# A router's gathering matrix from one comparison of counting products, with ranks and slots worked out afterwards

## The chip, the cores and the metric

The kernel runs on one core of a Trainium2 chip. The metric is the device time of one execution in microseconds (us); the time before is the median of three executions, 1223.32 us (1221.37 to 1224.46).

The engines of a core run their own instruction streams side by side and wait for each other through semaphores: TensorE (PE, matmuls; PEld is its weight load), VectorE (DVE), ScalarE (ACT), GpSimd (POOL) and SyncE (SP, which here only issues transfers). Transfers run on 16 DMA engines. PE writes its results to PSUM, DVE and ACT read them there and write to SBUF.

## The reference

One layer of a decoder trunk over 256 tokens of width 1024, all in float32. A token mixer (a gated linear attention branch and a short convolution branch) makes a new `x`. Then comes a mixture of experts:

```python
h   = RMSNorm(x) * (1 + scale2) + shift2
x   = x + gate2 * HierMoE(h)   # top-1 of 8 groups, then top-2 of 8 experts in the group
...
p_group = softmax(t @ rg_w + rg_b);  g_w, g_idx = top_k(p_group, 1)
e_logits = (t @ re_w + re_b).reshape(N, 8, 8)[group g_idx]
p_exp = softmax(e_logits);  e_w, e_loc = top_k(p_exp, 2)
e_w = e_w / sum(e_w) * g_w
out[token] += e_w * (silu(xb @ w1[e]) * (xb @ w3[e])) @ w2[e]
```

There are 64 experts of 6 MB of weights each (`w1`, `w3`: 1024 x 512, `w2`: 512 x 1024), and all of them are read. A final RMSNorm ends the layer.

## The kernel before

**The three stages.** First the token mixer (to about 297 us), whose weights come in blocks of 512 KB through a ring. Then the router: logits, top-1 group, top-2 experts, and for each token and choice a place in an expert's buffer. Then the experts, 16 groups of 4 experts (`EPG`), 12 units of 2 MB a group. Each expert has 32 slots (`CAP`), so that a group has 128 slots, one per column of a gathering matrix.

**The weight stream.** `Stream` holds the order of all transfers. SP issues the transfer of the next unit each time that the program is done with a unit (`st.done`) and so has a free buffer; the issue waits until PE has read the old unit for the last time. With all buffers asked for, eight transfers of 2 MB are outstanding at most.

**The router.** The logits are gathered in one PSUM tile (`pl`) by `x1_logits`, while the same blocks of `x` are transposed back to token rows; `ssq` holds the sums of squares. Then follow, as one chain of small operations: `rs` = 1/sqrt(mean square), logits `lg` = `pl` * `rs` + `rconst`, the maxima and their indices (`gm`, `gi`, `em`, `ei`), and `OO`, which holds for each token and choice a one at its expert (tokens x 2 halves x 2 choices x 64). ACT scales `acc` by `rs` to `h2`, the rows that will be gathered. The chain goes on:

- `osum` adds the two choices. Five small matmuls with `tri` (ones where the row is before the column) and `onesb` (ones) give `pc`: for each token and expert the number of tokens ahead that chose this expert, and in its third quarter the count of each expert.
- four instructions pick from `pc` the `rank` of each choice; `dst` = 32 * expert + rank (plus 8192 where the rank is 32 or more) is the place.
- two comparisons with a row of numbers (`io`) make `P1`, two more make and add `Pm`, the gathering matrix of group 0: tokens x 128 slots, a one where the token sits in the slot.
- `keep_warm` runs matmuls whose result nobody reads, 4 ahead of the counting matmuls and 2 behind them.

**Group 0.** Its eight first-layer units (`l1_unit`, u = 0 to 7) need the gathered columns `xg`; `gather_part` makes a quarter of them, four matmuls of `h2` with `Pm` into one PSUM tile and then two evacuations, which apply the norm's scale and shift: by ACT for the even quarters, by DVE for the odd ones. Quarter u is made just ahead of unit u for u = 0 to 3. After unit 3, `after_start` puts on DVE and ACT what the rest needs: the places in all groups (`dg`), `P1` of the second choice, the softmax weights (`weights`, six exponentials on ACT) and the tables for experts with more than 32 tokens (`overflow_tables`). After unit 5, `after_start2` makes the weighted matrix of group 0 by `slot_weights` (transposes on PE); it stands ahead of unit 6 on PE.

PSUM tiles named `m` come from a ring of four banks. One of the four holds `pl` until the experts begin; then the ring starts anew.

Of the kernel before, what the change touches and what calls it, by code (L numbers as in the profile page):

```python
# [27 lines left out]
LASTC = ((0, 512), (512, 256), (768, 128), (896, 128))  # L28
LASTN = (2, 2, 4, 4)
NB = 12  # L30
WARM = (4, 2)
# [65 lines left out]
def trunk_kernel(ctx: ExitStack, tc: tile.TileContext, xT: bass.AP, c: bass.AP, modw: bass.AP,  # L97
# [734 lines left out]
    assert not todo  # L832

    rs = sm.tile([128, 4], F32, name="rs")
    pl = L["pl"]
    V.tensor_reduce(rs[:, 2:4], ssq, axis=AX.X, op=OP.add)
    S.activation(rs[:, 0:2], rs[:, 2:4], AF.Sqrt, bias=epsc, scale=1.0 / D)
    V.reciprocal(rs[:, 0:2], rs[:, 0:2])
    o = [0]

    def scratch(*shape):
        n = 1
        for d in shape:
# [12 lines left out]
    OO = scratch(4, 64).rearrange("p (t k) e -> p t k e", t=2)  # L856
# [5 lines left out]
    xb, incl, excl = scratch(64), scratch(64), scratch(64)  # L862
    ovs = scratch(2, 2)
    cnt = scratch(64)
    osum = sm.tile([128, 2, 64], BF, name="osum")
# [13 lines left out]
    ebi = sm.tile([128, 3, 16], I32, name="ebi")  # L879

    for tt in range(TT):
        V.scalar_tensor_tensor(lg[:, tt], pl[:, tt, :72], rs[:, tt:tt + 1], rconst, op0=OP.mult, op1=OP.add)
    for tt in range(TT):
        V.max(gm[:, tt], lg[:, tt, :8])
    for tt in range(TT):
# [1 line left out]
    for tt in range(TT):  # L887
# [1 line left out]
    V.tensor_tensor(off8, io[:, None, :8].to_broadcast([128, 2, 8]), gi[:, :, 0:1].to_broadcast([128, 2, 8]),  # L889
                    op=OP.not_equal)  # L890
    V.scalar_tensor_tensor(lm.rearrange("p t (g e) -> p t g e", g=8), off8[:, :, :, None].to_broadcast([128, 2, 8, 8]),
                           -3.0e38, lg[:, :, 8:72].rearrange("p t (g e) -> p t g e", g=8), op0=OP.mult, op1=OP.add)
    for tt in range(TT):
        V.max(em[:, tt], lm[:, tt])
    for tt in range(TT):
        V.max_index(ei[:, tt], em[:, tt], lm[:, tt])
    V.tensor_tensor(OO, io[:, None, None, :64].to_broadcast([128, 2, 2, 64]),
                    ei[:, :, 0:2, None].to_broadcast([128, 2, 2, 64]), op=OP.is_equal)
    V.tensor_add(osum, O1, O2)
    V.tensor_scalar(dst, ei[:, :, 0:2], float(CAP), None, op0=OP.mult)  # L900
    keep_warm(WARM[0])
    pc = mt(4, 64)
    T.matmul(pc[:, 0], tri, osum[:, 0], start=True, stop=True)
    T.matmul(pc[:, 1], tri, osum[:, 1], start=True, stop=False)
    T.matmul(pc[:, 1], onesb, osum[:, 0], start=False, stop=True)
    T.matmul(pc[:, 2], onesb, osum[:, 0], start=True, stop=False)
    T.matmul(pc[:, 2], onesb, osum[:, 1], start=False, stop=True)
    keep_warm(WARM[1])
    for tt in range(TT):
        for k in range(2):  # L910
            V.scalar_tensor_tensor(prr[:, tt, k], pc[:, tt], 1.0, OO[:, tt, k], op0=OP.mult, op1=OP.mult,
                                   accum_out=rank[:, tt, k:k + 1])
    V.tensor_add(dst, dst, rank)
    V.tensor_scalar(big8, rank, float(CAP), 8192.0, op0=OP.is_ge, op1=OP.mult)
    V.tensor_add(dst, dst, big8)
    S.copy(cnt, pc[:, 2])
    pz_cm.__exit__(None, None, None)
    pa = ctx.enter_context(tc.tile_pool(name="pa", bufs=2, space=bass.MemoryType.PSUM))
    mring[:] = [(mring[0] + i) % 4 for i in range(4)]
    rot["m"] = 0  # L920

    def weights():
        V.tensor_scalar(nm[:, :, 0], gm[:, :, 0], -1.0, None, op0=OP.mult)
        V.tensor_scalar(nm[:, :, 1], em[:, :, 0], -1.0, None, op0=OP.mult)
        for tt in range(TT):
            S.activation(ex[:, 0:8], lg[:, tt, :8], AF.Exp, bias=nm[:, tt, 0:1], accum_out=zz[:, tt, 0:1])
            S.activation(ex, lm[:, tt], AF.Exp, bias=nm[:, tt, 1:2], accum_out=zz[:, tt, 1:2])
            S.activation(pw[:, tt], em[:, tt, 0:2], AF.Exp, bias=nm[:, tt, 1:2])
# [45 lines left out]
    def gather_part(xg, i):  # L974
        ps = mt(2, 128)
        for j in range(2):
            for tt in range(TT):
                f = 256 * i + 128 * j
                T.matmul(ps[:, j], h2[:, tt, f:f + 128], Pm[:, tt], start=(tt == 0), stop=(tt == 1))  # L979
        for j in range(2):  # L980
            k = 2 * i + j
            if i % 2 == 0:
                S.activation(xg[:, k], ps[:, j], AF.Identity, bias=B2[:, k:k + 1], scale=A2[:, k:k + 1])  # L983
            else:
                V.tensor_scalar(xg[:, k], ps[:, j], A2[:, k:k + 1], B2[:, k:k + 1], op0=OP.mult, op1=OP.add)  # L985

    def gather(key, i):
        X[key] = X["xg"][i % 2]
# [45 lines left out]
                T.matmul(ps[:, :w], pwt[:, tt], X["y"][:, s], start=True, stop=True)  # L1034
                V.tensor_add(acc[:, tt, s], acc[:, tt, s], ps[:, :w])  # L1035

    for tt in range(TT):
        V.tensor_scalar(P1[:, 0, tt], io, dst[:, tt, 0:1], None, op0=OP.is_equal)
    for tt in range(TT):
        V.scalar_tensor_tensor(Pm[:, tt], io, dst[:, tt, 1:2], P1[:, 0, tt], op0=OP.is_equal, op1=OP.add)  # L1040
    X["xg"] = [xt[:, i].rearrange("p (k s) -> p k s", k=KT) for i in range(2)]
    X["y"], X["g2r"] = xt[:, 2], xt[:, 3]
    X[0] = X["xg"][0]
# [63 lines left out]
    for g in range(NGRP):  # L1107
        if g == OVG:
            combine(g - 1)
            held = st.done(("e", g - 1, NU - 1), keep=True)  # L1110
            overflow(held)
            slots(g, dg, g)
            gather(g, g)
            slot_weights(g)
            st.free(held)
        ps = pa.tile([128, D], F32, name="a")
        for u in range(KT):
            if g == 0 and u < 4:
                gather_part(X[0], u)
            if g == last and u == 0:  # L1120
                S.dma_start(sq[0:1, :], bass.AP(tensor=fg.tensor, offset=fg.offset, ap=[[D, 1], [1, D]]))
            if g == last and u == 5:
                final_gain()
            l1_unit(ps, g, u, unit("e", g, u))
            st.done(("e", g, u))
            if g == 0 and u == 3:
                after_start()
            if g == 0 and u == 5:
                after_start2()
            if u == 2 and g > 0 and g != OVG:  # L1130
                combine(g - 1)
            if u == (4 if g else 6) and g + 1 < NGRP and g + 1 != OVG:
                slots(g + 1, dg, g + 1)
                gather(g + 1, g + 1)
                slot_weights(g + 1)
        act(ps)
        ps = pa.tile([128, D], F32, name="a")
        if g < last:
            for f in range(4):
                l2_unit(ps, f, unit("e", g, KT + f))  # L1140
                if not (g + 1 == OVG and f == 3):
                    st.done(("e", g, KT + f))
            evac_y(ps)
# [126 lines left out]
```

## Time and profile before

| | us |
|---|---|
| median of three executions | 1223.32 |
| the profiled execution | 1223.55 |
| its span | 1221.5 |
| PE busy | 907.0 (74%) |
| DVE busy | 378.1 (31%) |
| ACT busy | 224.2 (18%) |
| read from HBM over the span | 475.79 MB, 390 GB/s in the mean |

The span runs from the first to the last instruction on the engines. [...] In a row of the chain that ended last, a number is the start in us from the span's start and the next one how long this step held the end. In a row of a timeline the brackets say how long the engine sat idle before and what ended that.

### The profile page before, as it was taken

The page shows a single profiled execution, that of the slowest core. Times are in us where ns is not written, and L with a number is a line of the kernel's source. Part 1 is how long each engine was busy: PE and PEld are TensorE (multiplying, and loading weights), DVE is VectorE, ACT ScalarE, POOL GpSimd, SP SyncE. Part 2 cuts the span into 40 slices and gives each one's busy share as a digit, 9 for nine tenths or more (in the row PEclk, how much of TensorE's full clock was granted, in tenths as well). Part 3 has the DMA queues.
Part 4 walks back from the last instruction along what each step waited for, and adds up shares of the span by engine and source line. Part 5 has one row for each costly group of instructions (what it writes and reads, how often), then busy time and mean ns, then how long its engine had stood idle before and what let it go on. Part 6 is the DMA issues. An engine that isn't in the chain of part 4 may idle for free.

```text
span 1221.5 us, 14621 instructions
## 1 busy us (share of the span) xinstructions
PE 907.0 (74%) x6201; PEld 478.3 (39%) x6201; DVE 378.1 (31%) x716; ACT 224.2 (18%) x375; POOL 3.9 (0%) x15
## 2 busy tenths in 40 slices
PE   9999999999786757567666776665756665756565
PEld 6999999998332312121212121221212111412112
DVE  8967699664421202021111111111102010302003
ACT  6774445433201101010101010100000000100002
POOL 0000000000000000000000000000000000000000
PEclk9999999999899888897978778888889888989888
DMA  9997579978999999999999999999999999999996
GB/s 365 393 334 244 185 231 354 356 269 313 399 413 428 428 429 427 428 428 429 427 428 427 428 428 427 427 427 428 428 428 428 428 428 428 426 427 428 427 425 246
DMA packets 51337, 477.84 MB, mean 391 GB/s; under 512 B 5954, under 2 KB 6082, under 8 KB 27076
## 3 DMA queue, kind: packets, MB, share of 16 engines
q1 hardware_dynamic: 50400, 475.81, 94.9%
q8 instruction: 50, 0.82, 0.3%
q10 hardware_dynamic: 868, 1.05, 0.2%
q14 instruction: 19, 0.16, 0.0%
HBM read 475.79 MB, written 1.05 MB: 390 GB/s over the span
## 4 chain that ended last, share of the span: by engine, by line
DMA 67%; PE 29%; DVE 3%; ACT 1%; issue 0%; DVEq 0%; SPq 0%; ACTq 0%
DMA unit<-in_ew_dram 67%; PE z L331 17%; PE a L1007 3%; PE m L339 2%; PE z L348 2%; PE m L979 1%; PE m L1034 1%; PE a L1149 0%; PE z L199 0%; PE m L504 0%; PE m L481 0%; PE m L500 0%; PE m L271 0%; DVE xt L232 0%; DVE sp L322 0%
## 5 line engine op out<-in xcount | busy, mean ns | idle before, releaser
L1007 PE MATMUL a<-unit,xt 128*32 128x512 f32 x1424 | 204.8, 704 | 106.0 <-DMA unit<-in_ew_dram 105.4
L1007 PE MATMUL a<-unit,gt 128*32 128x512 f32 x672 | 112.0, 801 | 68.6 <-DMA unit<-in_ew_dram 63.3
L1007 PEld LDWEIGHTS a<-unit,xt 128*32 128x32 f32 x1424 | 44.1, 120 | 257.0 <-DMA unit<-in_ew_dram 131.9
L331 PE MATMUL z<-hhl,sp 128*128 128x256 f32 x1152 | 140.9, 284 | 0.0
L331 PEld LDWEIGHTS z<-hhl,sp 128*128 128x128 f32 x1152 | 138.9, 192 | 1.6 <-issue 1.5
L983 ACT ACTIVATE xt<-m,modc,A 128x128 f32<-128x128 f32 x64 | 25.9, 454 | 534.9 <-PE m L979 534.9
L1007 PE MATMUL a<-ring,xt 128*32 128x512 f32 x624 | 91.6, 714 | 38.4 <-DMA ring<-in_ew_dram 38.4
L322 DVE TENSOR_TENSOR sp<-ring,sp 128x1024 fp32r<-128x1024 f32 x88 | 106.8, 1219 | 42.8 <-ACT sp L315 41.1
L315 ACT CAST sp<-ring 128x1024 fp32r<-128x1024 f32 x88 | 91.5, 1048 | 97.7 <-PE z L331 68.2
L1035 DVE TENSOR_TENSOR wk<-wk,m 128x512 f32<-128x512 f32 (+2 forms) x68 | 44.5, 656 | 205.4 <-PE m L1034 205.4
L1025 DVE TENSOR_TENSOR xt<-a,xt 128x1024 f32<-128x1024 f32 (+3 forms) x19 | 20.0, 1055 | 268.8 <-PE a L1007 261.9
L1007 PEld LDWEIGHTS a<-unit,gt 128*32 128x32 f32 x672 | 21.8, 127 | 140.8 <-DMA unit<-in_ew_dram 86.5
L1034 PE MATMUL m<-xt,pwt 128*128 128x512 f32 (+2 forms) x136 | 64.1, 613 | 5.3 <-DVE xt L1025 5.3
L979 PEld LDWEIGHTS m<-Pm,wk 128*128 128x128 f32 x512 | 58.6, 192 | 19.8 <-issue 19.8
L1015 DVE TENSOR_TENSOR gt<-gt,a 128x512 f32<-128x512 f32 x16 | 11.0, 688 | 175.7 <-ACT gt L1014 175.7
L979 PE MATMUL m<-Pm,wk 128*128 128x128 f32 x512 | 62.2, 279 | 3.4 <-DVE Pm L972 3.1
L1007 PE MATMUL a<-ring,gt 128*32 128x512 f32 x288 | 44.4, 745 | 25.7 <-DMA ring<-in_ew_dram 25.6
L232 DVE SCALAR_TENSOR_TENSOR xt<-ring,xt 128x1024 f32<-128x1024 f32 x48 | 58.5, 1219 | 0.4
L1007 PEld LDWEIGHTS a<-ring,xt 128*32 128x32 f32 x624 | 18.2, 120 | 97.5 <-DMA ring<-in_ew_dram 62.5
L985 DVE TENSOR_SCALAR xt<-m,A,modc 128x128 f32<-128x128 f32 x64 | 23.3, 405 | 106.2 <-PE m L979 106.2
L1034 PEld LDWEIGHTS m<-xt,pwt 128*128 128x128 f32 x136 | 25.8, 205 | 50.2 <-issue 37.6
L1014 ACT ACTIVATE gt<-a 128x512 f32<-128x512 f32 x16 | 9.6, 597 | 184.3 <-PE a L1007 184.3
(252 smaller groups left out, 634.0 us busy)
## 6 DMA issues: line engine op xcount, KB each, us to landing
unit<-in_ew_dram SPq DMA_DIRECT2D x131, 2048.0 KB, 39.1
ring<-in_ew_dram SPq DMA_DIRECT2D x54, 2048.0 KB, 39.1
ring<-in_win_dram SPq DMA_DIRECT2D x88, 512.0 KB, 8.3
ring<-in_modw_dram SPq DMA_DIRECT2D x48, 512.0 KB, 7.0
ring<-in_ew_dram SPq DMA_DIRECT2D x12, 512.0 KB, 4.8
unit<-in_el_dram SPq DMA_DIRECT2D x4, 1024.0 KB, 34.8
unit<-in_el_dram SPq DMA_DIRECT2D x4, 512.0 KB, 18.6
ring<-in_el_dram SPq DMA_DIRECT2D x4, 512.0 KB, 12.5
```

What stands on the lines that cost most here:

```text
L232: V.scalar_tensor_tensor(scr, st.block("m", i, b), 1.0, cB, op0=OP.mult, op1=OP.mult, accum_out=modc[:, 4 * i + b:4 * i + b + 1])
L315: S.copy(sp(b)[:, 0], st.block("w", n, i))
L322: V.tensor_sub(t[:, 1], st.block("w", n, i), t[:, 0].bitcast(F32))
L331: T.matmul(ps, t[:, ws, k], rhs[rs][:, k], start=(clear and k == 0 and n == 0), stop=(k == KT - 1 and n == 2), skip_group_check=True)
L339: T.matmul(pb[:, h % 2], t[:, ws, h], hl[rs][:, kk], start=(kk == 0 and h % 2 == 0 and n == 0), stop=(kk == KT - 1 and h % 2 == 1 and n == ...
L348: T.matmul(pv[tt][hh], hl[rs][:, kk, 128 * tt:128 * tt + 128], t[:, ws, 512 * hh:512 * hh + 512], start=(kk == 0 and n == 0), stop=(kk == ...
L979: T.matmul(ps[:, j], h2[:, tt, f:f + 128], Pm[:, tt], start=(tt == 0), stop=(tt == 1))
L983: S.activation(xg[:, k], ps[:, j], AF.Identity, bias=B2[:, k:k + 1], scale=A2[:, k:k + 1])
L985: V.tensor_scalar(xg[:, k], ps[:, j], A2[:, k:k + 1], B2[:, k:k + 1], op0=OP.mult, op1=OP.add)
L1007: T.matmul(ps[32 * j:32 * j + 32, 512 * hh:512 * hh + 512], lhsT[:, 32 * j:32 * j + 32], w[:, j, 512 * hh:512 * hh + 512], start=first, st ...
L1034: T.matmul(ps[:, :w], pwt[:, tt], X["y"][:, s], start=True, stop=True)
L1035: V.tensor_add(acc[:, tt, s], acc[:, tt, s], ps[:, :w])
```

## The change

The logits are no longer divided by the root: `lg` is now `rconst` * root + `pl`, the root (`std`) being what ACT gives, and `rs` is made behind it; the exponentials take `rs` as their scale. The counting matmuls take the two choices of `OO` (now bfloat16) one after the other instead of their sum, and their matrix `trif` has -8192 (`FAR`) on its diagonal, so that a token's count for an expert that it did choose is its rank - 8192, and 0 or more otherwise. One comparison of `pc` with the slot numbers - 8192 (`iof`) gives `Pm` of group 0. Ranks, places and counts (`places`) are worked out behind it, and `P1` in `after_start`. The first quarter of the gathering uses two PSUM tiles instead of one. In `x1_logits` both transposes stand ahead of both logit matmuls. The 2 matmuls of `keep_warm` behind the counting are gone.

```diff
     def x1_logits(k, pt):
         for tt in range(TT):
+            T.transpose(pt(tt), xres[:, k, 128 * tt:128 * tt + 128], ident)
+        for tt in range(TT):
             s = slice(128 * tt, 128 * tt + 128)
-            T.transpose(pt(tt), xres[:, k, s], ident)
             T.matmul(L["pl"][:, tt, :72], xres[:, k, s], wrt[:, k], start=(k == 0 and tt == 0),
...
-    S.activation(rs[:, 0:2], rs[:, 2:4], AF.Sqrt, bias=epsc, scale=1.0 / D)
-    V.reciprocal(rs[:, 0:2], rs[:, 0:2])
+    S.activation(std, rs[:, 2:4], AF.Sqrt, bias=epsc, scale=1.0 / D)
...
-        V.scalar_tensor_tensor(lg[:, tt], pl[:, tt, :72], rs[:, tt:tt + 1], rconst, op0=OP.mult, op1=OP.add)
+        V.scalar_tensor_tensor(lg[:, tt], rconst, std[:, tt:tt + 1], pl[:, tt, :72], op0=OP.mult, op1=OP.add)
+    V.reciprocal(rs[:, 0:2], std)
...
-    V.tensor_add(osum, O1, O2)
-    V.tensor_scalar(dst, ei[:, :, 0:2], float(CAP), None, op0=OP.mult)
-    keep_warm(WARM[0])
+    keep_warm(WARM)
     pc = mt(4, 64)
-    T.matmul(pc[:, 0], tri, osum[:, 0], start=True, stop=True)
...
-    keep_warm(WARM[1])
     for tt in range(TT):
-        for k in range(2):
-            V.scalar_tensor_tensor(prr[:, tt, k], pc[:, tt], 1.0, OO[:, tt, k], op0=OP.mult, op1=OP.mult,
-                                   accum_out=rank[:, tt, k:k + 1])
-    V.tensor_add(dst, dst, rank)
...
+        sums = [(trif, tt)] + [(onesb, 0)] * tt
+        for n, (w, t) in enumerate(sums):
+            for k in range(2):
+                T.matmul(pc[:, tt], w, OO[:, t, k], start=(n == 0 and k == 0), stop=(n == tt and k == 1))
+    for n in range(4):
+        T.matmul(pc[:, 2], onesb, OO[:, n // 2, n % 2], start=(n == 0), stop=(n == 3))
+
+    def places():
+        V.tensor_scalar(dst, ei[:, :, 0:2], float(CAP), None, op0=OP.mult)
+        for tt in range(TT):
+            for k in range(2):
+                V.scalar_tensor_tensor(prr[:, tt, k], pc[:, tt], FAR, OO[:, tt, k], op0=OP.add, op1=OP.mult,
+                                       accum_out=rank[:, tt, k:k + 1])
+        V.tensor_add(dst, dst, rank)
+        V.tensor_scalar(big8, rank, float(CAP), 8192.0, op0=OP.is_ge, op1=OP.mult)
+        V.tensor_add(dst, dst, big8)
+        S.copy(cnt, pc[:, 2])
...
-            S.activation(ex, lm[:, tt], AF.Exp, bias=nm[:, tt, 1:2], accum_out=zz[:, tt, 1:2])
+            S.activation(ex, lm[:, tt], AF.Exp, bias=nm[:, tt, 1:2], scale=r, accum_out=zz[:, tt, 1:2])
...
-        ps = mt(2, 128)
+        if split:
+            ps = [mt(128) for _ in range(2)]
+        else:
+            both = mt(2, 128)
+            ps = [both[:, j] for j in range(2)]
...
-    for tt in range(TT):
-        V.tensor_scalar(P1[:, 0, tt], io, dst[:, tt, 0:1], None, op0=OP.is_equal)
-    for tt in range(TT):
-        V.scalar_tensor_tensor(Pm[:, tt], io, dst[:, tt, 1:2], P1[:, 0, tt], op0=OP.is_equal, op1=OP.add)
+    V.tensor_tensor(Pm.rearrange("p t (j s) -> p t j s", j=EPG), pc[:, 0:2, 0:EPG, None].to_broadcast([128, TT, EPG, CAP]),
+                    iof[:, None, None, :].to_broadcast([128, TT, EPG, CAP]), op=OP.is_equal)
+    places()
...
-        for tt in range(TT):
-            V.tensor_scalar(P1[:, 1, tt], io, dst[:, tt, 1:2], None, op0=OP.is_equal)
+        for k in range(2):
+            for tt in range(TT):
+                V.tensor_scalar(P1[:, k, tt], io, dst[:, tt, k:k + 1], None, op0=OP.is_equal)
...
-                gather_part(X[0], u)
+                gather_part(X[0], u, u == 0)
```

The first place where instructions move is DVE between `OO` and the gathering of group 0. These are its rows before (`xt` holds the small scratch tiles, `m` is `pc`, `P_113` is `P1`):

```order
L897 TENSOR_TENSOR xt<-io,xt 128x256 [waits DVE_49]
L899 TENSOR_TENSOR osum<-xt 128x128 [waits DVE_49]
L900 TENSOR_SCALAR dst<-xt 128x4
L911 SCALAR_TENSOR_TENSOR xt,rank<-m,xt 128x64 [waits PE_49]
L911 SCALAR_TENSOR_TENSOR xt,rank<-m,xt 128x64 x3
L913 TENSOR_TENSOR dst<-dst,rank 128x4 [waits DVE_49]
L914 TENSOR_SCALAR xt<-rank 128x4
L915 TENSOR_TENSOR dst<-dst,xt 128x4 [waits DVE_49]
L1038 TENSOR_SCALAR P_113<-io,dst 128x128 [waits DVE_49]
L1038 TENSOR_SCALAR P_113<-io,dst 128x128
L1040 SCALAR_TENSOR_TENSOR Pm<-io,dst,P_113 128x128 [waits DVE_49] x2
```

And these are the rows of the same place in the changed kernel:

```order
L903 TENSOR_TENSOR OO<-io,xt 128x256 [waits DVE_49]
L1052 TENSOR_TENSOR Pm<-m,iof 128x256 [waits PE_49]
L917 TENSOR_SCALAR dst<-xt 128x4
L920 SCALAR_TENSOR_TENSOR xt,rank<-m,OO 128x64 [waits DVE_49]
L920 SCALAR_TENSOR_TENSOR xt,rank<-m,OO 128x64 x3
L922 TENSOR_TENSOR dst<-dst,rank 128x4 [waits DVE_49]
L923 TENSOR_SCALAR xt<-rank 128x4
L924 TENSOR_TENSOR dst<-dst,xt 128x4 [waits DVE_49]
```

`Pm` stands right behind `OO` with only PE's counting between them, and the ranks stand behind `Pm`; the four comparisons with `io` are gone from here.

The second place is PE from the last counting matmul to the first expert unit. Before (`wk` is `h2`, `z` the unread result of `keep_warm`):

```order
L907 MATMUL m<-osum,onesb 128x64
L870 MATMUL z<-xt,ident 128x512 x2
L979 MATMUL m<-Pm,wk 128x128 [waits DVE_49,Activation_49] x2
L979 MATMUL m<-Pm,wk 128x128 x2
L1007 MATMUL a<-unit,xt 32x512 [waits DMAHW7_49,Activation_49]
```

And in the changed kernel:

```order
L913 MATMUL m<-OO,onesb 128x64
L994 MATMUL m<-Pm,wk 128x128 [waits DVE_49,Activation_49]
L994 MATMUL m<-Pm,wk 128x128 [waits Activation_49] x2
L994 MATMUL m<-Pm,wk 128x128
L1022 MATMUL a<-unit,xt 32x512 [waits DMAHW7_49,Activation_49]
```

The third gathering matmul, the first into the second PSUM tile, has a wait for ACT of its own. In the built program it waits for the copy of the counts (`cnt`), since the second tile is the bank of `pc`; that copy waits for the fourth rank instruction on DVE; and the comparison that makes `Pm` waits for the last of all ten counting matmuls.

The third place is DVE in `after_start`. Before:

```order
L1046 TENSOR_TENSOR dg<-dst,iog 128x64
L1049 TENSOR_SCALAR P_113<-io,dst 128x128 x2
L923 TENSOR_SCALAR xt<-xt 128x2
L924 TENSOR_SCALAR xt<-xt 128x2
L929 RECIPROCAL xt<-xt 128x4 [waits Activation_49]
```

In the changed kernel (`P_117` is `P1`):

```order
L1060 TENSOR_TENSOR dg<-dst,iog 128x64 [waits DVE_49]
L1064 TENSOR_SCALAR P_117<-io,dst 128x128 x4
L934 SCALAR_TENSOR_TENSOR xt<-xt,rs 128x2 x2
L940 RECIPROCAL xt<-xt 128x4 [waits Activation_49]
```

Two comparisons more stand ahead of the two small instructions for which the exponentials on ACT wait.

## Rows read from the trace of the kernel before

**Rows 1.** The page's shares of the chain that ended last, by engine
```profile
DMA 67%; PE 29%; DVE 3%; ACT 1%; issue 0%; DVEq 0%; SPq 0%; ACTq 0%
```

**Rows 2.** Stretches: busy PE, PEld, DVE, ACT, POOL; granted clock, DMA share, GB/s
```profile
305.00:310.00 5.00, 4.15 (x32) 2.20 (x31) 0.77 (x4) 0.81 (x2) 0.00 (x0) 1.00 0.76 324
310.00:315.00 5.00, 5.00 (x44) 2.00 (x42) 0.73 (x2) 1.62 (x3) 0.00 (x0) 1.00 0.96 341
325.00:330.00 5.00, 1.83 (x8) 1.54 (x9) 4.53 (x16) 0.37 (x1) 0.00 (x0) 0.68 1.00 426
```

**Rows 3.** SP's issues in short windows, and the time to landing in each
```profile
L86 SPq DMA_DIRECT2D unit<-in_ew_dram x2: 328/376/423, 297.3 to 297.7; - x2
DMA to landing us min/median/max: 8.2/10.5/12.7
...
L86 SPq DMA_DIRECT2D unit<-in_ew_dram x1: 328/328/328, 309.4 to 309.4; - x1
...
L86 SPq DMA_DIRECT2D ring<-in_ew_dram x1: 327/327/327, 312.3 to 312.3; - x1
DMA to landing us min/median/max: 10.5/10.5/10.5
...
L86 SPq DMA_DIRECT2D unit<-in_ew_dram x1: 327/327/327, 334.2 to 334.2; - x1
DMA to landing us min/median/max: 13.5/13.5/13.5
...
L86 SPq DMA_DIRECT2D unit<-in_ew_dram x1: 328/328/328, 343.5 to 343.5; - x1
DMA to landing us min/median/max: 9.8/9.8/9.8
```

**Rows 4.** The chain that ended last, from the root to the first expert unit
```profile
299.82 0.18 DVE rs L838
...
300.11 0.49 DVE xt L882 x2
...
302.44 0.43 DVE xt L897
...
302.90 0.30 DVE osum L899
...
303.43 0.03 PE m L904
...
303.59 0.68 DVE xt L911 x8
...
305.65 1.18 PE m L979 x8
...
306.86 0.47 ACT xt L983
...
307.37 1.92 PE a L1007 x16
```

**Rows 5.** Timeline around the router: logit matmuls, scaling of `h2`, copy of the counts
```profile
298.08 0.34 PE L654 MATMUL m<-gt,xt 128*128 128x72 f32 x2
...
300.03 2.19 ACT L888 ACTIVATE wk<-wk,rs 128x1024 f32<-128x1024 f32 x2 [0.23 <-DVE rs L838]
...
304.34 0.21 ACT L916 COPY xt<-m 128x64 f32<-128x64 f32 x1 [2.13 <-DVE xt L911]
```

**Rows 6.** `after_start`: the chain's comparisons, and the timeline where PE's wait ends
```profile
317.17 0.39 DVE P L1049 x2
...
328.06 1.06 PE L999 MATMUL m<-ident,P 128*128 128x128 f32 x2 [6.51 <-DVE P L995]
```

**Rows 7.** ACT with a scale per partition and without, ns min/median/max of one
```profile
L259 ACT ACTIVATE A<-modc,b,colt x8: 380/382/387, 12.3 to 49.5; 128x1 f32<-128x1 f32 x8
...
L262 ACT ACTIVATE modc<-modc,colt x8: 278/294/297, 12.6 to 50.8; 128x1 f32<-128x1 f32 x8
```

**Rows 8.** Timeline: the last first-layer unit of all
```profile
1190.22 3.51 PE L1007 MATMUL a<-unit,xt 128*32 128x512 f32 x16 [2.98 <-DMA unit<-in_ew_dram]
```

More of the change, by code (lines that the diff above doesn't have):

```diff
@@ L30 @@
 NB = 12
-WARM = (4, 2)
+WARM = 4
+FAR = 8192.0
 START = (2, 2, 0, 2, 8)
@@ L213, in trunk_kernel @@
     V.tensor_scalar(tri, jp, 0.0, None, op0=OP.is_gt)
+    trif = sm.tile([128, 128], BF, name="trif")
+    V.scalar_tensor_tensor(trif, ident, -FAR, tri, op0=OP.mult, op1=OP.add)
     io = sm.tile([128, 128], F32, name="io")
     G.iota(io, pattern=[[1, 128]], base=0, channel_multiplier=0, allow_small_or_imprecise_dtypes=True)
+    iof = sm.tile([128, CAP], F32, name="iof")
+    V.tensor_scalar(iof, io[:, :CAP], FAR, None, op0=OP.subtract)
     iog = sm.tile([128, NGRP + 4], F32, name="iog")
@@ L834, in trunk_kernel @@
     rs = sm.tile([128, 4], F32, name="rs")
+    std = sm.tile([128, TT], F32, name="std")
     pl = L["pl"]
     V.tensor_reduce(rs[:, 2:4], ssq, axis=AX.X, op=OP.add)
-    S.activation(rs[:, 0:2], rs[:, 2:4], AF.Sqrt, bias=epsc, scale=1.0 / D)
-    V.reciprocal(rs[:, 0:2], rs[:, 0:2])
+    S.activation(std, rs[:, 2:4], AF.Sqrt, bias=epsc, scale=1.0 / D)
     o = [0]
@@ L855, in trunk_kernel @@
     em, ei = scratch(2, 8), scratch(2, 8).bitcast(U32)
-    OO = scratch(4, 64).rearrange("p (t k) e -> p t k e", t=2)
+    OO = sm.tile([128, 2, 2, 64], BF, name="OO")
     O1, O2 = OO[:, :, 0], OO[:, :, 1]
@@ L864, in trunk_kernel @@
     cnt = scratch(64)
-    osum = sm.tile([128, 2, 64], BF, name="osum")
     def keep_warm(n):
@@ L891, in trunk_kernel @@
     V.scalar_tensor_tensor(lm.rearrange("p t (g e) -> p t g e", g=8), off8[:, :, :, None].to_broadcast([128, 2, 8, 8]),
-                           -3.0e38, lg[:, :, 8:72].rearrange("p t (g e) -> p t g e", g=8), op0=OP.mult, op1=OP.add)
+                           -3.0e35, lg[:, :, 8:72].rearrange("p t (g e) -> p t g e", g=8), op0=OP.mult, op1=OP.add)
     for tt in range(TT):
@@ L898, in trunk_kernel @@
                     ei[:, :, 0:2, None].to_broadcast([128, 2, 2, 64]), op=OP.is_equal)
-    V.tensor_add(osum, O1, O2)
-    V.tensor_scalar(dst, ei[:, :, 0:2], float(CAP), None, op0=OP.mult)
-    keep_warm(WARM[0])
+    keep_warm(WARM)
     pc = mt(4, 64)
-    T.matmul(pc[:, 0], tri, osum[:, 0], start=True, stop=True)
[L904 to L907, printed above, removed]
-    keep_warm(WARM[1])
-    for tt in range(TT):
-        for k in range(2):
-            V.scalar_tensor_tensor(prr[:, tt, k], pc[:, tt], 1.0, OO[:, tt, k], op0=OP.mult, op1=OP.mult,
-                                   accum_out=rank[:, tt, k:k + 1])
-    V.tensor_add(dst, dst, rank)
-    V.tensor_scalar(big8, rank, float(CAP), 8192.0, op0=OP.is_ge, op1=OP.mult)
-    V.tensor_add(dst, dst, big8)
-    S.copy(cnt, pc[:, 2])
+    for tt in range(TT):
+        sums = [(trif, tt)] + [(onesb, 0)] * tt
[14 more added lines that the diff above has]
+        S.copy(cnt, pc[:, 2])
     pz_cm.__exit__(None, None, None)
@@ L922, in weights @@
     def weights():
-        V.tensor_scalar(nm[:, :, 0], gm[:, :, 0], -1.0, None, op0=OP.mult)
-        V.tensor_scalar(nm[:, :, 1], em[:, :, 0], -1.0, None, op0=OP.mult)
+        for i, top in enumerate((gm, em)):
+            V.scalar_tensor_tensor(nm[:, :, i], top[:, :, 0], -1.0, rs[:, 0:2], op0=OP.mult, op1=OP.mult)
         for tt in range(TT):
-            S.activation(ex[:, 0:8], lg[:, tt, :8], AF.Exp, bias=nm[:, tt, 0:1], accum_out=zz[:, tt, 0:1])
-            S.activation(ex, lm[:, tt], AF.Exp, bias=nm[:, tt, 1:2], accum_out=zz[:, tt, 1:2])
-            S.activation(pw[:, tt], em[:, tt, 0:2], AF.Exp, bias=nm[:, tt, 1:2])
+            r = rs[:, tt:tt + 1]
+            S.activation(ex[:, 0:8], lg[:, tt, :8], AF.Exp, bias=nm[:, tt, 0:1], scale=r, accum_out=zz[:, tt, 0:1])
+            S.activation(ex, lm[:, tt], AF.Exp, bias=nm[:, tt, 1:2], scale=r, accum_out=zz[:, tt, 1:2])
+            S.activation(pw[:, tt], em[:, tt, 0:2], AF.Exp, bias=nm[:, tt, 1:2], scale=r)
         V.reciprocal(zz, zz)
@@ L972, in slots, with gather_part @@
         V.tensor_add(Pm, P1[:, 0], P1[:, 1])
-    def gather_part(xg, i):
-        ps = mt(2, 128)
+    def gather_part(xg, i, split=False):
+        if split:
[3 more added lines that the diff above has]
+            ps = [both[:, j] for j in range(2)]
         for j in range(2):
@@ L978, in gather_part @@
                 f = 256 * i + 128 * j
-                T.matmul(ps[:, j], h2[:, tt, f:f + 128], Pm[:, tt], start=(tt == 0), stop=(tt == 1))
+                T.matmul(ps[j], h2[:, tt, f:f + 128], Pm[:, tt], start=(tt == 0), stop=(tt == 1))
         for j in range(2):
@@ L982, in gather_part @@
             if i % 2 == 0:
-                S.activation(xg[:, k], ps[:, j], AF.Identity, bias=B2[:, k:k + 1], scale=A2[:, k:k + 1])
+                S.activation(xg[:, k], ps[j], AF.Identity, bias=B2[:, k:k + 1], scale=A2[:, k:k + 1])
             else:
-                V.tensor_scalar(xg[:, k], ps[:, j], A2[:, k:k + 1], B2[:, k:k + 1], op0=OP.mult, op1=OP.add)
+                V.tensor_scalar(xg[:, k], ps[j], A2[:, k:k + 1], B2[:, k:k + 1], op0=OP.mult, op1=OP.add)
     def gather(key, i):
```

## The prediction

> **What bounds the kernel now.** I read the shares of the chain that ended last first: DMA holds two thirds of the span [rows 1], and PE is still waiting for a weight transfer 31 us before the end [rows 8]. So the experts run at the pace of the weight stream, and work between two landings costs nothing. What the router costs is read from the stream itself: how long do the DMA engines stand still while the router holds back the release of buffers?
>
> The stretches show it: in 305 to 310 us they are busy for 0.76 of the time, in 310 to 315 us they move 341 GB/s, against 426 GB/s in a full stretch such as 325 to 330 us [rows 2]. The issues with their landings tell how much that is [rows 3]. A unit of 2.1 MB takes 4.9 us at the full rate. The unit issued at 297.7 us lands at 310.4. The next one can't be issued before unit 0 of group 0 is used up, at 309.4 us. The one behind it, issued at 312.3, lands at 322.8, so the one of 309.4 landed at about 318.0 if the two lie 4.9 apart: 7.6 us behind 310.4 where 4.9 would do. **2.7 us of the stream are lost at the router.** There is a second, smaller loss: the unit of 334.2 lands at 347.7, the next one, issued at 343.5, at 353.3, which is 5.6 behind: 0.7 us lost. An issue with more than 5 us of work ahead of it in the queue (312.3: 318.0 - 312.3 = 5.7) lost nothing; with 4.2 us left (343.5) it lost 0.7, with 1.0 us left (309.4) it lost 2.7. I read a line through these: about 0.65 us lost for each us by which the work left falls short of 5.2.
>
> So the most that any change of the router alone can bring is 2.7 + 0.7 = 3.4 us, which is 0.28% of the time.
>
> **The change part by part.** The sum follows the chain from the root to the first expert unit [rows 4].
>
> *Logits from the root.* The reciprocal starts at 299.82 and the logits at 300.11. Now the logits start where the reciprocal did, 0.29 earlier, but the reciprocal stands behind them on DVE and takes between nothing and its own 0.18 from the maxima. I take 0.1, so the gain is 0.2 and the comparison that makes `OO` moves from 302.44 to 302.24. ACT's scaling of `h2` gets `rs` some 0.4 us later; its 2.19 us began at 300.03 [rows 5], now end at 302.65, and have the time until the gathering at 303.8 (below) as cover. The transposes' new order could let the last sums of squares start earlier by at most the pair of logit matmuls that stood in front, 0.34 [rows 5]; DVE is busy with its own copies and squares there, so I take 0.
>
> *Counting without the sum.* `OO` to `osum` is 302.44 to 302.90, so `OO` is there 0.46 after its start. From `osum` (302.90) to the first reader of the counts (303.59) it takes 0.69, of which the sum itself is 0.30; the launch and five matmuls are 0.39. Five more matmuls at 0.03 each make 0.54. The new comparison starts at 302.24 + 0.46 + 0.54 = 303.24. It waits for all ten matmuls, although it reads nothing of the last four. [...]
>
> *One comparison.* The trace has no comparison of this size that reads PSUM with each number repeated; the nearest is that of `OO`, of as many elements, 0.46 to its reader. I take 0.46 and a launch of 0.1, and the gathering starts at 303.8 instead of 305.65. It could take up to a quarter of a us more.
>
> *The split quarter.* The first half of the gathering takes half of the 1.18 us. The second half writes into the bank of `pc` and waits for the copy of the counts, which waits for the ranks: `places` runs behind the comparison, from about 303.75 with the small instruction ahead of it, its four rank instructions take 0.68 as before [rows 4], and the copy 0.21 and launches of 0.1 [rows 5], so 304.7. Then half a gathering, 0.55: 305.25. ACT's evacuation of the first half also stands behind the copy and reaches PE 0.51 after its start (306.86 to 307.37), at 305.2. **Unit 0 starts at 305.25 instead of 307.37: 2.1 us earlier**, and so does every issue up to 321.6 us. With the split and no wait it would be 304.9.
>
> *The stall behind unit 5.* PE stands still for 6.51 us until DVE has done `after_start` [rows 6], so what is added there is on PE's path. Two comparisons at 0.2 each [rows 6] are 0.4. Five exponentials, up to the last one that DVE waits for, get a scale per partition; the nearest rows are 0.38 with one and 0.29 without [rows 7], so 0.09 each or 0.45 (bounds 0, if ACT overlaps it, and 0.9, twice that). So 0.85 of the 2.1 goes back to the stall, and the issues of 334.2 and 343.5 come **1.25 us earlier**. At the issue of 334.2 the stream still has 8.5 us of work left (the landing before lies 4.9 ahead of 347.7, at 342.8), so nothing is lost there; what the stall gives or takes counts at the issue of 343.5.
>
> *In the stream.* The issue of 309.4 moves to 307.3, with 3.1 us of work left: by the line it loses 1.35 instead of 2.7 and lands 1.35 earlier. The landing before 353.3 is 1.35 earlier too, the issue of 343.5 is 1.25 earlier, the work left stays at 4.1, the loss at 0.7: **1.3 us earlier in all**, and from there landing follows landing to the end. If instead the first issue lands a fixed 8.6 us after it, it gains the whole 2.1, and the end 0.35 x 2.1 + 0.65 x 1.25 = 1.55, or all 2.1 where the line is too steep. With 0.9 for the exponentials and 0.25 for the comparison the end gains 0.8. So the gain is 0.8 to 2.1, and I take 1.3.
>
> The profiled execution took 1223.55 us for a span of 1221.5, and the median of the runs is 0.23 less than it. 1223.55 - 1.3 - 0.23 = **1222.0 us**. That is 0.1%; less than 0.3% (3.7 us) can't be told from no change here, the three runs of one kernel lie 3.1 us apart.
>
> **The rivals.** (1) *The gain stops at the second gate.* If the stall grows by more than 2 us (the exponentials dearer than twice the rows, `places` late on DVE), the issue of 343.5 is not earlier at all and 0.35 x 1.35 = 0.5 us is left: 1222.8. For it speaks that this issue is the last one with too little work ahead; against it, that everything added on that path is small.
>
> [...]
>
> (3) *Faster by more than the router gives: the tail.* The last first-layer unit ran at about half clock, 3.51 instead of 1.92 us [rows 8], behind the last wait for the stream, where every us counts. If a shift of the stream against the clock's changes spares it, the end gains 1.6 more, and about as much again if the next units are spared as well: 1222.0 - 3.2 = 1218.8. Nothing says that it will.
>
> (4) *The change does nothing that reaches the end*, since the first issue's landing is set by something else than its issue: 1223.3.
>
> **How the numbers follow.** Forecast (gain 0.8 to 2.1) 0.58; rivals 1 and 4 together 0.22; rival 2 0.10; rival 3 0.10. The forecast and rivals 1 and 4 are within 0.3%, as is rival 2 up to 1227.0; I give half of it to slower. Of rival 3 some 0.07 is past 3.7 us. So faster 0.07, same 0.88, slower 0.05. The range for 8 in 10 takes in the forecast's own 1221.2 to 1222.5, rivals 1 and 4, and the nearer parts of rivals 2 and 3: 1219.4 to 1224.4.
>
> **What would show each step.** The chain of the changed kernel should have `Pm`'s comparison at about 303.2, the first gathering matmul at 303.8 and unit 0 at 305.2; the third gathering matmul should wait for ACT. The wait of PE behind unit 5 should be near 7.4 us, and the issues now at 309.4, 334.2 and 343.5 at 307.3, 332.9 and 342.2. The landing now at 318.0 should be at 316.7, the one at 353.3 at 352.0. The granted clock should be 1.00 from 300 to 320 us. The prediction is wrong if the clock falls there, if the landing at 353 us doesn't move, or if it moves and the span doesn't follow: then something behind the stream's last landing took it back.

## The result, and the profile after

The changed kernel takes **1215.77 us** (median of 7 runs, 1214.56 to 1218.99) beside 1222.91 us before (7 runs), ratio **0.9948 [0.9937, 0.9960]**: 0.5% faster, 6 us below the forecast and outside the range. The profiled execution took 1218.99 us for a span of 1216.9, the longest of the seven, so its trace shows less of the gain than the median does: 4.6 us of span.

First the router. The timeline of the kernel after (a row: start, duration, engine, line, operation; in brackets the idle time before it and what ended that) answers to [rows 4 to 6, 8]:

```profile
298.89 0.29 ACT L844 ACTIVATE std<-rs,epsc 128x2 f32<-128x2 f32 x1 [0.48 <-DVE rs L843]
...
301.61 0.42 DVE L903 TENSOR_TENSOR OO<-io,xt 128x256 bf16<-128x256 f32 x1
302.09 0.28 PE L911 MATMUL m<-OO,trif 128*128 128x64 bf16 x4 [0.28 <-DVE OO L903]
...
302.58 0.42 DVE L1052 TENSOR_TENSOR Pm<-m,iof 128x256 f32<-128x256 f32 x1 [0.54 <-PE m L913]
...
303.15 0.68 PE L994 MATMUL m<-Pm,wk 128*128 128x128 f32 x4 [0.61 <-DVE Pm L1052]
...
303.73 0.21 ACT L925 COPY xt<-m 128x64 f32<-128x64 f32 x1 [1.67 <-DVE xt L920]
...
304.00 0.71 PE L994 MATMUL m<-Pm,wk 128*128 128x128 f32 x4 [0.17 <-ACT xt L925]
...
304.64 1.92 PE L1022 MATMUL a<-unit,xt 128*32 128x512 f32 x16
...
315.33 0.39 ACT L937 ACTIVATE xt<-xt,rs 128x8 f32<-128x8 f32 x1 [2.59 <-DVE xt L934]
...
326.19 1.06 PE L1014 MATMUL m<-ident,P 128*128 128x128 f32 x2 [7.36 <-DVE P L1010]
...
1185.67 3.58 PE L1022 MATMUL a<-unit,xt 128*32 128x512 f32 x16 [2.92 <-DMA unit<-in_ew_dram]
```

The root, ahead of everything that the change touches in the router, already stands 0.61 us earlier than in the trace before, where it is

```profile
299.50 0.30 ACT L837 ACTIVATE rs<-rs,epsc 128x2 f32<-128x2 f32 x1 [0.63 <-DVE rs L836]
```

The change can't be shown to do that: over the traces of this study the root stands between 298.3 and 299.7 us, with the changed router at 298.50 to 299.47 and without it at 298.30 to 299.65. So times near the router are compared from the root. Unit 0 starts 304.64 - 298.89 = 5.75 us behind it, against 7.87 before (307.37 - 299.50): 2.12 us earlier, where the prediction had 2.1.

Next the stream behind the router, which answers to [rows 2]: stretches of the kernel after (busy time of PE, PEld, DVE, ACT, POOL; granted clock, which is the share of full speed that TensorE was given; DMA share, GB/s).

```profile
305.00:310.00 5.00, 5.00 (x45) 2.21 (x38) 0.73 (x2) 0.20 (x1) 0.00 (x0) 1.00 0.98 390
310.00:315.00 5.00, 5.00 (x46) 2.33 (x48) 1.43 (x7) 2.09 (x3) 0.00 (x0) 1.00 0.99 416
325.00:330.00 5.00, 3.71 (x18) 2.36 (x22) 2.95 (x13) 1.54 (x3) 0.00 (x0) 0.50 0.99 424
...
340.00:350.00 10.00, 7.91 (x40) 2.03 (x36) 0.69 (x1) 1.18 (x2) 0.00 (x0) 0.52 0.92 349
350.00:360.00 10.00, 10.00 (x90) 2.90 (x83) 1.23 (x1) 0.00 (x0) 0.00 (x0) 1.00 0.96 378
```

At the router the hole is nearly gone: 390 and 416 GB/s where 324 and 341 stood. But a new one opens between 340 and 360 us, with the granted clock at 0.52 in 340 to 350 us and 1.00 in 350 to 360. In the kernel before those two stretches have a clock of 0.83 and 1.00:

```profile
340.00:350.00 10.00, 7.91 (x57) 2.21 (x60) 0.69 (x1) 1.55 (x3) 0.00 (x0) 0.83 1.00 408
350.00:360.00 10.00, 10.00 (x84) 3.21 (x77) 1.73 (x2) 0.00 (x0) 0.00 (x0) 1.00 0.99 405
```

SP's issues of the kernel after, with the time to landing [rows 3], say the same; the last one is the first issue behind the pause at the second layer:

```profile
L87 SPq DMA_DIRECT2D unit<-in_ew_dram x1: 328/328/328, 332.6 to 332.6; - x1
...
DMA to landing us min/median/max: 12.0/12.0/12.0
...
L87 SPq DMA_DIRECT2D unit<-in_ew_dram x1: 328/328/328, 341.5 to 341.5; - x1
...
DMA to landing us min/median/max: 10.8/10.8/10.8
...
L87 SPq DMA_DIRECT2D ring<-in_ew_dram x1: 328/328/328, 364.8 to 364.8; - x1
...
DMA to landing us min/median/max: 28.9/28.9/28.9
```

The counterpart of that last issue in the kernel before:

```profile
L86 SPq DMA_DIRECT2D ring<-in_ew_dram x1: 328/328/328, 364.0 to 364.0; - x1
...
DMA to landing us min/median/max: 28.7/28.7/28.7
```

The unit of 332.6 lands at 344.6, 3.1 us before its counterpart (347.7); the next one at 352.3, only 1.0 before (353.3); and the one of 364.8 at 393.7, 1.0 us *behind* its counterpart (364.0 and 28.7 us under way, so 392.7). **At 393 us the profiled kernel after is later than the kernel before; at the last first-layer unit, 1185.67 against 1190.22 [rows 8], it is 4.55 us earlier.** The gain arises in the steady stream in between, where the change alters no instruction's order. There the page on transfers says, for 400 to 1100 us, before and after:

```profile
DMA packets 20557, 299.37 MB, mean 428 GB/s; under 512 B 2283, under 2 KB 2283, under 8 KB 2283
...
unit<-in_ew_dram SPq DMA_DIRECT2D x99, 2048.0 KB, 39.2
```

```profile
DMA packets 20690, 301.37 MB, mean 431 GB/s; under 512 B 2294, under 2 KB 2294, under 8 KB 2294
...
unit<-in_ew_dram SPq DMA_DIRECT2D x100, 2048.0 KB, 38.8
```

301.37 / 299.37 is 0.67% more in the same time. The records of the single packets in the two traces (a transfer is 128 packets of 16 KB) agree: in these 700 us such a packet took 615.9 ns in the mean before and 612.2 after. Over the 793 us from 393 to 1186 that is 5.3 us; less the 1.0 lost by 393 it is 4.3 of the 4.55. The chain that ended last [rows 1] can't be set beside it, since in the trace after it is followed back only to about 1041 us.

### The profile page after: what moved, and what is told of

Its sections match the earlier page's. It is cut to its first block, busy times and chain, and to the rows that moved or that the text cites. A ratio compares the mean times of both kernels' runs of the same rounds, so it can differ in the third digit from the quotient of the medians.

```text
span 1216.9 us, 14623 instructions
## 1 busy us (share of the span) xinstructions
PE 905.3 (74%) x6202; PEld 479.9 (39%) x6202; DVE 377.7 (31%) x716; ACT 224.8 (18%) x375; POOL 3.9 (0%) x15
## 5 line engine op out<-in xcount | busy, mean ns | idle before, releaser
L1022 PE MATMUL a<-ring,xt 128*32 128x512 f32 x624 | 85.6, 671 | 36.4 <-DMA ring<-in_ew_dram 36.4
L1022 PE MATMUL a<-ring,gt 128*32 128x512 f32 x288 | 48.1, 801 | 30.4 <-DMA ring<-in_ew_dram 30.4
## 6 DMA issues: line engine op xcount, KB each, us to landing
unit<-in_ew_dram SPq DMA_DIRECT2D x131, 2048.0 KB, 38.8
ring<-in_ew_dram SPq DMA_DIRECT2D x54, 2048.0 KB, 38.8
```

What stands on the lines that cost most here:

```text
L1022: T.matmul(ps[32 * j:32 * j + 32, 512 * hh:512 * hh + 512], lhsT[:, 32 * j:32 * j + 32], w[:, j, 512 * hh:512 * hh + 512], start=first, st ...
```

## The experiments

**The theories.** The change makes new small tiles: `trif` (256 bytes of each partition), `iof` (128), `std` (32 with its padding) and `OO` (512), and drops `osum` (256). So everything allocated behind them, the ring and the units into which the stream writes, moves up by 672 bytes: in the built programs the ring's start goes from byte 31584 of a partition, 96 past a multiple of 256, to 32256, a multiple of 512, and every unit's start, which lies whole multiples of 512 behind it, likewise. *Theory:* the stream is faster because of where its buffers start. *Rival:* the gain comes from the router after all, by an issue order that fills the stream better, and the rate goes with it.

Each of the kernels e1 to e6 shifts the buffers by lengthening one small tile and does nothing else; n is the number of bytes over 4:

```diff
-    Pm = sm.tile([128, TT, 128], F32, name="Pm")
+    Pm = sm.tile([128, TT * 128 + n], F32, name="Pm")[:, :TT * 128].rearrange("p (t s) -> p t s", t=TT)
```

**e1**, the kernel before, n = 168.

> The kernel before with 672 bytes per partition of unused space behind Pm, so that the weight buffers start at the addresses of the changed kernel (a multiple of 512 bytes instead of 32 past a multiple of 64); no instruction differs. Address theory (the stream is faster because of where its buffers lie): stream at 430 to 431 GB/s instead of 427 to 428, and 4 to 6 us faster than before, near 1218 us. Router theory (the gain comes from the earlier release of buffers): no change, 1222.9 us within 1 us, stream at 428 GB/s.

Measured: 1217.25 us, ratio 0.9949 [0.9935, 0.9963] to the kernel before of the same series (1223.37 us): 6.1 us. The kernel before with nothing but its buffers moved has the changed kernel's whole gain (0.9948).

**e2**, the kernel after, n = 88: its ring at 32608, 96 past a multiple of 256 as before.

> The changed kernel with 352 bytes of unused space behind Pm, so that the weight buffers start 32 bytes past a multiple of 64, as before; no instruction differs from the changed kernel. Address theory: the stream falls back to 427 to 428 GB/s and 4 to 6 us are lost, 1220 to 1222 us, and what is left against the kernel before, 1 to 3 us, is the router's part. Router theory: 1215.8 us as the changed kernel.

Measured: 1222.40 us, ratio 0.9996 [0.9986, 1.0006]. The router's change without the shift makes no difference that can be measured; 1 to 3 us were expected of it. The transfers of e1 and e2, 400 to 1100 us, as above:

```profile
DMA packets 20692, 301.37 MB, mean 431 GB/s; under 512 B 2296, under 2 KB 2296, under 8 KB 2296
```

```profile
DMA packets 20552, 299.34 MB, mean 428 GB/s; under 512 B 2280, under 2 KB 2280, under 8 KB 2280
```

The rate follows the address and not the router. The rival falls. Nor did the engines become faster: in these 700 us DVE and ACT are busy for 101.26 and 38.06 us in the kernel before, for 101.31 and 38.05 in e1, and the granted clock is 0.85 and 0.83.

**e3** and **e4**, the kernel before, n = 8 (31616, a multiple of 128) and n = 24 (31680, a multiple of 64).

> The kernel before with 32 bytes of unused space behind Pm: the weight buffers start at a multiple of 128 bytes that is none of 256. If what counts is a multiple of 64 (or 128) bytes: 430 GB/s and as fast as with 672 bytes. If it must be a multiple of 256 or 512: 428 GB/s and 1222.9 us. Router theory: 1222.9 us.

> The kernel before with 96 bytes of unused space behind Pm: the weight buffers start at a multiple of 64 bytes that is none of 128. If a multiple of 64 is enough: as fast as with 672 bytes, near 1218 us. If it must be 128 or more: 1222.9 us. Router theory: 1222.9 us.

Measured: e3 1223.24 us, 1.0000 [0.9990, 1.0010]; e4 1223.75 us, 1.0004 [0.9993, 1.0014]; 428 and 427 GB/s. Neither 64 nor 128 is enough, and how far the start lies off (96, 128 or 192 bytes) makes no difference.

**e5** and **e6**, the kernel before, n = 104 (32000, a multiple of 256 and not of 512) and n = 40 (31744, a multiple of 1024).

> The kernel before with 416 bytes more in the small pool: the big buffers (ring and units) start at byte 32000 of a partition, a multiple of 256 but not of 512 (before: 31584; in the run moved by 672 bytes: 32256, a multiple of 512). Theory A (a write into a buffer on a 256-byte boundary is what is faster): ratio 0.993 to 0.9965 of the kernel before, as in the run moved by 672, and 430 to 431 GB/s between 400 and 1100 us. Theory B (512 bytes are needed): ratio 0.998 to 1.002 and 427 to 428 GB/s, as in the runs moved by 32 and by 96. A third outcome, about 0.997 to 0.998 and 429 GB/s, would say that the gain comes in steps.

> The kernel before with 160 bytes more: the big buffers start at byte 31744, a multiple of 1024. Theory A (256 bytes) and theory B (512 bytes) both expect ratio 0.993 to 0.9965 and 430 to 431 GB/s, no more than at 32256. A theory by which each doubling of the boundary brings more expects under 0.993 and 432 GB/s or more. Theory C (no boundary at all: the gain came from the smaller free space or from which tiles lie above 32 KB) expects a ratio of 0.998 to 1.002, since this kernel's buffers start below 32256.

Measured: e5 1216.66 us, 0.9950 [0.9935, 0.9965], 431 GB/s; e6 1215.87 us, 0.9940 [0.9924, 0.9955], 430 GB/s. Of the powers of two 256 is the boundary; 512 and 1024 bring nothing more that can be told apart.

**e8**, the kernel before, where only the big tiles behind `xt` move: the seven buffers of the units and one tile of rows into which no weights go (`wk`), but neither the ring nor a small tile.

```diff
-    xt = big.tile([128, 4, 1024], F32, name="xt", tag="T5")
+    xt = big.tile([128, 4 * 1024 + 40], F32, name="xt", tag="T5")[:, :4096].rearrange("p (a b) -> p a b", a=4)
```

> The kernel before, where the tile xt alone is 160 bytes longer: all small tiles, the ring and xt stay where they were (ring at 31584), and only the big tiles behind xt, the units among them, move, to a 256-byte boundary (97280). Theory A (the stream's rate follows the boundary of the buffer that a transfer writes): of the 143 transfers between 400 and 1100 us 100 go to units, so 0.7 of the gain of 0.52%: ratio 0.995 to 0.9975 and 429.5 to 430 GB/s. Rival (the place of the small tiles or of the ring makes the gain): ratio 0.999 to 1.001 and 427 to 428 GB/s.

Measured: 1218.14 us, ratio 0.9956 [0.9941, 0.9971], and for 400 to 1100 us

```profile
DMA packets 20687, 301.29 MB, mean 430 GB/s; under 512 B 2296, under 2 KB 2296, under 8 KB 2296
```

So the place of a small tile isn't what counts. DVE's and ACT's busy times are again those of the kernel before (101.34 and 38.07 us), so what is left is the start of the units' buffers. But the theory in its simple form, by which each transfer pays for the buffer that it writes, missed: it would give 0.7 of the gain, 300.8 MB, as 43 of the 143 transfers still go to the ring, 96 bytes off the boundary. Moved were 301.29 MB, nearly all of the gain (e1: 301.37), and the packet records show no slow ones: 99% of the 16 KB packets took 611 ns, as with all buffers on the boundary (over 99% in the kernel after); in the kernel before 13% did. The time can't tell the two apart: its interval holds both 0.7 of the gain and all of it. The ring alone was not moved.

**e7**: the other question is why the router's gain was gone at 360 us. The kernel after gets unread matmuls in PE's wait of 7.36 us, to see whether the clock then stays up there (FILL = 14):

```diff
     def after_start2():
+        fill = mt(512)
+        for _ in range(FILL):
+            T.matmul(fill, ident, h2[:, 0, 0:512], start=True, stop=True)
         slot_weights(0)
```

> The changed kernel (buffers at 32256, 512-byte boundary) with 14 more matmuls, 128 by 512, whose results nobody reads, in TensorE's wait behind unit 5 (7.36 us in the changed kernel's profile; at 0.46 us each they fill 6.4 us of it). Theory: the router's 2.1 us were lost between 325 and 355 us, where the granted clock fell to 0.73 and 0.68 and the slices before the units were late; with the wait filled the clock of 325 to 340 us is 0.85 or more, 340 to 355 us comes back to 390 GB/s or more (342 in the changed kernel's profile), and the median is 1212 to 1215 us, ratio to the kernel before 0.990 to 0.994, below the changed kernel's 0.9948. Rival: the clock falls there anyway or the second gate (the slot weights) holds the issues of 343 us where they are: 1215 to 1218 us, ratio 0.994 to 0.997. Second rival: the matmuls end later than VectorE's slot weights and push unit 6: over 1218 us.

Measured: 1217.19 us, 0.9948 [0.9936, 0.9960]. The 14 were twice too many: each shows as two matmuls of 0.44 us, they fill 12.28 us, and unit 6 starts at 332.64 instead of 328.88.

```profile
319.34 12.28 PE L1073 MATMUL m<-wk,ident 128*128 128x512 f32 x28
...
332.64 1.92 PE L1023 MATMUL a<-unit,xt 128*32 128x512 f32 x16
```

The clock stayed at 1.00 from 325 to 355 us, and yet 340 to 355 us moved only 389 GB/s. The time is the first rival's and not the theory's (1212 to 1215 us); since the push makes the issues late by itself, the run doesn't decide between them. So **e9** has FILL = 7, and **e10** is e1 with the same seven matmuls.

> The changed kernel with 7 unread matmuls ahead of the slot weights instead of 14 (one took 0.44 us for each of its two passes, so 14 filled 12.28 us and pushed unit 6 by 3.8 us; 7 fill 6.15 of the 7.36 us). Theory (the clock's fall behind the wait gives back the router's gain): granted clock 1.00 from 325 to 355 us, the issue that stood at 332.58 us stays within 0.5 us of it, 340 to 355 us moves 415 GB/s or more instead of 342, so 2.5 us of the stream come back: median 1213 to 1215 us, ratio 0.991 to 0.994. Rival (the loss of 340 to 355 us isn't the clock's): under 380 GB/s there with the clock at 1.00, and ratio 0.994 to 0.997 as without the matmuls.

> The kernel before with its big buffers at 32256 and the same 7 unread matmuls in its wait of 6.51 us behind unit 5. Beside e9 it shows what the router change is worth where neither the boundary nor the clock differ. If the prediction's sum holds there (1.3 us to the end at a clock that doesn't fall), this one is 0.5 to 2 us above e9; if the second gate takes all of it, the two are within 0.5 us.

Measured: e9 **1214.77 us** (1214.40 to 1216.75), 0.9933 [0.9918, 0.9949]; e10 1215.96 us (1215.33 to 1217.09), 0.9938 [0.9923, 0.9952]. Stretches of e9, as above:

```profile
325.00:340.00 15.00, 10.29 (x80) 6.28 (x80) 5.81 (x21) 4.51 (x10) 0.00 (x0) 1.00 1.01 428
340.00:350.00 10.00, 9.84 (x92) 3.02 (x96) 1.23 (x1) 0.10 (x1) 0.00 (x0) 1.00 1.00 429
350.00:360.00 10.00, 10.00 (x68) 3.38 (x61) 3.96 (x9) 0.00 (x0) 0.00 (x0) 1.00 1.01 430
```

With the wait filled the clock is 1.00 (0.73 in 325 to 340 us and 0.52 in 340 to 350 in the kernel after) and the second hole is gone: 429 and 430 GB/s where the kernel after had 349 and 378. The way from the clock to the hole is the lateness of the issues. These are unit 6 and the start of the next five issues, first in the kernel after and then in e9:

```profile
328.88 3.64 PE L1022 MATMUL a<-unit,xt 128*32 128x512 f32 x16
...
332.58 20.25 SPq L87 DMA_DIRECT2D unit<-in_ew_dram  x5
```

```profile
327.52 1.92 PE L1023 MATMUL a<-unit,xt 128*32 128x512 f32 x16
...
329.50 16.40 SPq L88 DMA_DIRECT2D unit<-in_ew_dram  x5
```

The issue was expected to stay within 0.5 us of 332.58, but counted from the root it comes 2.7 us earlier, since PE's work between the wait and the issue isn't slowed (unit 6 takes 1.92 us instead of 3.64). That work is the same, so in this pair the lateness, and with it the hole, was the clock's, against the rival. The end is less clear: the ratios of e9 and of the changed kernel overlap, so the fill's own gain in time isn't shown.

What the router's change is worth in that state is read from e9 and e10: the timeline's root and unit 0, and the first issue behind the second layer's pause with its landing; e9 first.

```profile
298.50 0.29 ACT L845 ACTIVATE std<-rs,epsc 128x2 f32<-128x2 f32 x1 [0.48 <-DVE rs L844]
...
304.25 1.92 PE L1023 MATMUL a<-unit,xt 128*32 128x512 f32 x16
...
L88 SPq DMA_DIRECT2D ring<-in_ew_dram x1: 328/328/328, 357.9 to 357.9; - x1
...
DMA to landing us min/median/max: 31.0/31.0/31.0
```

```profile
299.24 0.30 ACT L838 ACTIVATE rs<-rs,epsc 128x2 f32<-128x2 f32 x1 [0.63 <-DVE rs L837]
...
307.12 1.92 PE L1008 MATMUL a<-unit,xt 128*32 128x512 f32 x16 [0.55 <-ACT xt L984]
...
L87 SPq DMA_DIRECT2D ring<-in_ew_dram x1: 327/327/327, 359.9 to 359.9; - x1
...
DMA to landing us min/median/max: 30.9/30.9/30.9
```

From the root, unit 0 stands at 5.75 and 7.88 us: 2.13 earlier. The landing stands at 388.9 - 298.5 = 90.4 and 390.8 - 299.24 = 91.6: **1.2 us earlier**, and the medians differ by 1.2. The runs of the two overlap, so of the end itself this is no proof. And it is one trace of each: on the way the lead stands between 0.8 us (the landings of 345.3 and 346.8) and 1.6 (those of 320.2 and 322.5), and from 384 us on between 1.0 and 1.2.

## Why the prediction was wrong

**The step that failed** is the frame and not a term of the sum. "A unit of 2.1 MB takes 4.9 us at the full rate" and "from there landing follows landing to the end" took the stream's rate as a constant of the kernel, and the change was costed only where it alters instructions. It also alters addresses. The forecast put 0 on that, none of the rivals was it, and by itself it was worth 6.1 us in e1, the whole ratio of the change; e2, without it, kept nothing that can be measured. The bound of 3.4 us held for the router's work but not for the change.

**The router.** From the root its steps came out as written. With 0.61 us added, the root's lead, the comparison starts at 303.19 (303.2 forecast), the first gathering matmul at 303.76 (303.8), unit 0 at 305.25 (305.25); the third gathering matmul waited for ACT's copy, which waited for the ranks. PE's wait was 7.36 us (7.4), its exponentials 0.39 (the estimate: 0.38 with a scale). Ten counting matmuls and the comparison had the durations taken. Rival 2, which has 0.10 of the chances and reaches up to 1227.0 us, is a clock that falls at the router; no run shows that fall or its cost: from 300 to 320 us the granted clock was 1.00 in the trace after, as before.

**The stream behind it.** Two terms were right where the clock didn't fall and wrong where it did. In the filled pair the gain at the landing was 1.2 us from the root, and 1.3 was forecast. That the sizes meet is in part luck: in that pair the second gate cost nothing (e9's second issue, at 337.4 us, had 7.9 us of work ahead of it), where the forecast has it cost 0.7 on both sides. In the profiled kernel after, the loss at the issue near 342 us was 2.9 us (352.3 - 344.6 = 7.7, less 4.8 to 4.9 for a unit), against a forecast of "the loss at 0.7". The step that failed there is "the work left stays at 4.1": it was 344.6 - 341.5 = 3.1, as the unit ahead landed 3.1 us earlier and the issue moved by only 2.0. By the prediction's own line 3.1 us left would cost 1.4, so the line failed there too; of its three points the one without a loss was assumed and not read, since the landing at 318.0 was set 4.9 us ahead of the next. And from 340 to 350 us, with that issue at 341.5, the clock was at 0.52; in the same trace unit 6 took 3.64 us at 0.51, and unit 0 took 1.92 at 1.00. A clock of 0.68 in 325 to 330 us, around the end of PE's wait of 6.51 us, stood in the rows of before [rows 2, 6], but the sum took its cost as constant. So the router's gain was lost at the gate that rival 1 names, though not by its cause, a longer wait, and by more than it said: at 393 us, counted from the root, the profiled kernel after is 94.8 us along (393.7 - 298.89), the kernel before 93.2 (392.7 - 299.50). Up to 344.6 us it had been 2.5 us ahead; 2.1 of the 4.1 go by the landing of 352.3, and the rest, by that of 393.7, isn't followed to its cause here. e2, the change without the shift, came out at no difference, with an interval that holds the forecast's 1.3 us (0.9989) too.

**The tail** [rows 8]. Its unit ran in 3.58 us at a granted clock of 0.52, before in 3.51 us at 0.53; rival 3 didn't happen.

**What stays open.** Why the granted clock was lower behind the wait in the trace after (0.52 in 340 to 350 us) than before (0.83): in e2 it was 0.78, and without the router's change 0.68 in e1 and 1.00 in e4 and e5, which have no fill either. So it varies between runs, and one profile of each can't tell whether the change shifts it. Nor does the clock of that stretch alone set the hole's depth: e1 moved 411 GB/s there at 0.68, e2 with the router's change 360 at 0.78. That two of the changed kernel's seven runs lie near 1218.9 us and five at 1214.6 to 1215.9 would suit this loss, but only one of the two is profiled. It wasn't tried whether the filled wait gains without the shift. And how the start of a buffer slows the stream is not shown (last section): PE reads the same buffers, and no run moves its reads apart from the writes.

## What to carry to other kernels

Ask of every change what it does to the addresses of the buffers that a bound stream writes: here 672 bytes more ahead of them in a pool were worth 6.1 us (e1). Where a transfer stream sets the time, try its buffers on a multiple of 256 bytes in the partition (430 to 431 GB/s here, 427 to 428 off it), and compare variants only at equal placement, since otherwise a neutral edit can show a gain or a loss that isn't its own (ratio 0.9949 in e1). A gain ahead of a wait is worth what is left of it behind the wait: from the root 2.13 us at unit 0 and 1.2 at the landing behind the second layer's pause (e9 and e10). Where the clock fell behind the wait (0.52 in 340 to 350 us), seven unread matmuls that end before the wait does kept it at 1.00 here (e9), and the stream full with it, at 429 GB/s; what they bring at the end must be measured.

## What the runs showed of the hardware

The start of the destination in a partition changed the rate of a saturated stream, with the sizes and the order of the transfers unchanged: 427 to 428 GB/s at 96, 128 and 192 bytes past a multiple of 256 (before, e2, e3, e4), 430 to 431 at 0 (after, e1, e5, e6), and 430 with the units at 0 and the ring at 96 (e8). In the time of the kernel that is 0.5 to 0.6%, and 0.4% in e8.

The loss doesn't grow with the distance from the boundary: from 400 to 1100 us the starts at 96, 128 and 192 bytes moved 299.37, 299.35 and 299.24 MB (before, e3, e4), each 0.7% less than the 301.37 of e1. Of a transfer the written side alone moved in these runs.

Two readings of the packet records speak against a fixed cost of each packet off the boundary. In e8 the packets into the ring aren't slower; its transfers into the ring and into the units both took 38.8 us from issue to landing in the median, where those of the kernel before took 39.2. And in the kernel before, whose buffers all lie 96 bytes off, the median packet took 611 ns in 330 to 350 us and 612 in 370 to 390, beside 611 in the kernel after; only from 390 us on, where eight transfers are outstanding and 39 us pass from issue to landing, did more than half take 613 ns or more. What the start of a buffer does to a full stream is shown by its effect, then; the mechanism stays open.

The second thing is how much a fall of the clock in PE's wait weighs although the stream still had transfers outstanding: in e9 seven unread matmuls, 6.28 us of work that nobody needs, went with a clock of 1.00 and 429 GB/s in 340 to 350 us, where the kernel after had 0.52 and 349.
